# Taking the first norm's sums of squares from a second, untransposed copy of the input

## The chip, the cores and the metric

One core of one Trainium2 chip. The metric is device time in microseconds (us) of one execution; the kernel before takes 523.28 us (median of 3 runs, 523.22 to 523.72). Everything is float32; the large matmuls run in a split form described below.

## The reference, cut to what matters

One layer of an encoder trunk on 512 tokens of width 1024:

```
h    = rms_norm(x, attn_norm_g)            # x * rsqrt(mean(x*x) + 1e-6) * g, per token
proj = h @ w_in                            # 1024 x 2560: [xr | gate | q | k | v]
xr   = conv4(xr) -> RG-LRU scans, * gelu(gate);  q, k, v -> dilated attention
x    = x + concat(norm(y_rnn), norm(y_attn)) @ w_out
x    = x + relu(norm(x) @ w_up)^2 @ w_down
out  = rms_norm(x, final_norm_g)
```

The change concerns the first line alone: the 512 numbers mean(x*x), one per token.

## The kernel before, in words

**Layout.** The host passes x twice: transposed with weights beside it (`xw0`, `xw`: eight pieces of 128 channels x 512 tokens, each with 384 columns of `w_in`), and with tokens on partitions (`xn`, eight pieces of 128 tokens x 512 channels), which the kernel before reads only later, for the residual. The projection puts channels on the contracted dimension, so it works on the transposed copy. The norm's factor per token (`rstd`) is not multiplied into x; it is applied to the projections when they leave PSUM. So the matmuls can begin before the sums of squares are known.

**Split matmuls.** Every large product is three matmuls of a high part and a low part (`mm3`, lines 312 to 314). The high part is a rounded copy (ScalarE, line 247 for a chunk of weights, `conv_hi`; VectorE for a few chunks, line 245), the low part is the difference (VectorE, line 269, `conv_lo`).

**The opening.** `cvx(k)` (lines 353 to 367) splits piece k of x and of the weights beside it. `sq(k)` (line 372) squares the piece on ScalarE, `addsq` (line 375) adds the squares over the eight pieces on VectorE. TensorE meanwhile runs three output tiles of the projection over k (`pxr`, lines 453 and 458); after the first triple of the last k it turns the 128 x 512 sum of squares with four transposes (`turned`, line 430). VectorE sums the turned tile along its rows (line 435), scales it (line 414), POOL raises it to the power -1/2 (line 417, `rcol`), TensorE spreads it to a row with four more transposes (`row_tile`, line 409), ScalarE copies it out of PSUM (line 423, `rrow`, which is `rstd`).

**What hangs on `rstd`.** `conv_a(t)` (lines 496, 498) scales a `pxr` tile by it and begins the width-4 convolution, `conv_b(t)` (lines 503 to 505) ends it; both for t = 0 to 3. VectorE runs them one after the other. `lru_gates` (lines 528, 532) then multiplies each convolved tile by four small gate matrices on TensorE, in order of t, and ScalarE evacuates them. Between, TensorE runs the fourth `pxr` tile (`xmm`, chunk 3 of the weights) and the gate projections (`pp`, chunk 4 onward, one chunk a tile).

**Order.** TensorE, ScalarE, VectorE and POOL issue in the order of the program (a hand-written schedule). The transfers of SyncE's queue (SP) are placed by the framework's scheduler: seven pieces of x and weights, the vectors `vt`, piece 7 (it reuses the buffer of piece 0, so it waits until that piece has been read), weight chunks 3, 4 and 5 (`emit_dma`, line 230; three buffers, which pieces 4 to 6 of x occupy first), then the four gate matrices (line 320), then chunks 6 and 7 as buffers come free. ScalarE splits chunk 3, then chunk 5, and only then copies out `rrow`; chunk 4's high part is VectorE's.

Of the kernel before, what the change touches and what calls it, by code (L numbers as in the profile page):

```python
# [12 lines left out]
FT = mybir.dt.float32  # L13
FR = mybir.dt.float32r
AF = mybir.ActivationFunctionType
OP = mybir.AluOpType

P = 128
S = 512
D = 1024  # L20
KD = D // P
# [77 lines left out]
def hybrid_kernel(ctx: ExitStack, tc, xw0, xw, xn, w_in, w_v, w_out, w_up, w_dn, gates, vecs, bias, fg, out):  # L99
    nc = tc.nc  # L100
    consts = ctx.enter_context(tc.tile_pool(name="consts", bufs=1))
# [7 lines left out]
    act = nc.scalar.activation  # L109
    stt = nc.vector.scalar_tensor_tensor  # L110
    NG = 45

    def g_(name, dt=FT, shape=(P, S)):
        return work.tile(list(shape), dt, name=name, tag="g", bufs=NG)

    def small(name, w):
        return work.tile([P, w], FT, name=name, tag="sm%d" % w, bufs=8)

    def ps_(name, tag):
        return psum.tile([P, S], FT, name=name, tag=tag, bufs={"pj": 4, "gs": 2, "et": 2}[tag])  # L120

    def f(t):
        return t.bitcast(FT)


    vt = consts.tile([P, NVEC], FT, name="vt")
# [6 lines left out]
    ident = consts.tile([P, P], FT, name="ident")  # L133
# [10 lines left out]
    def softplus_consts():  # L144
        ts, tt = nc.gpsimd.tensor_scalar, nc.gpsimd.tensor_tensor
        lam = vt[:, VEC["lam"]:VEC["lam"] + 8]
        e8, sp, z, z2, pl = [small(n, 8) for n in ("e8", "sp8", "z8", "z28", "pl8")]
        cneg = consts.tile([P, 8], FT, name="cneg")
        chalf = consts.tile([P, 8], FT, name="chalf")
        stt(e8, lam, -1.0, lam, op0=OP.mult, op1=OP.max)  # L150
        nc.vector.tensor_scalar(sp, lam, -1.0, 0.0, op0=OP.mult, op1=OP.max)
        yield
        act(e8, e8, AF.Exp, scale=-1.0)
        yield
        nc.vector.tensor_scalar(z, e8, 2.0, None, op0=OP.add)
        nc.vector.reciprocal(z, z)
        tt(z, z, e8, op=OP.mult)
        tt(z2, z, z, op=OP.mult)
        ts(pl, z2, 1.0 / 19, 1.0 / 17, op0=OP.mult, op1=OP.add)
        for c in (15, 13, 11, 9, 7, 5, 3, 1):  # L160
            if c == 7:
                yield
            tt(pl, pl, z2, op=OP.mult)
            ts(pl, pl, 1.0 / c, None, op0=OP.add)
        tt(pl, pl, z, op=OP.mult)
        ts(pl, pl, 2.0, None, op0=OP.mult)
        tt(sp, pl, sp, op=OP.add)
        ts(cneg, sp, -LRU_C, None, op0=OP.mult)
        ts(chalf, sp, 0.5 * LRU_C, None, op0=OP.mult)
        yield cneg, chalf  # L170

    spc = softplus_consts()
# [38 lines left out]
    def source(c):  # L211
        if not isinstance(c, tuple):
            return c
        if c[0] == "o":
            return oblock(c[1])
        return ublock(*c[:3]) if len(c) == 4 else wblock(*c)
# [9 lines left out]
    def emit_dma():  # L226
        if plain:
            i = plain.popleft()
            r = stream.tile([P, 1024], FT, name="wraw", tag="wraw", bufs=3)
            nc.sync.dma_start(r, source(chunks[i]))  # L230
            raws[i] = r
# [86 lines left out]
    def gate_load(t):  # L318
        gwr[t] = g_("gwr", shape=(P, 4 * DH))
        nc.sync.dma_start(gwr[t], gates[t])  # L320


    h_hi = big.tile([P, KD, S], FR, name="h_hi", tag="bigA")
    h_lo = big.tile([P, KD, S], FR, name="h_lo", tag="bigB")

    XW, XG = S + 3 * P, S + KD
    ag = consts.tile([P, KD], FT, name="ag")
    xwt, w3 = [], []
    for k in range(KD):
        if 4 <= k < 7:  # L330
            xwt.append(stream.tile([P, 1024], FT, name="wraw", tag="wraw", bufs=3)[:, :XW])
        else:
            xwt.append(work.tile([P, 1024], FT, name="tw", tag="tw", bufs=4)[:, :XW if k else XG + 3 * P])
        if k == 0:
            nc.sync.dma_start(xwt[0][:, :XG], xw0[:, :XG])
            nc.sync.dma_start(xwt[0][:, XG:], xw0[:, XG:])
            nc.gpsimd.tensor_copy(ag, xwt[0][:, S:XG])
            w03 = g_("w03")[:, :P]
            nc.sync.dma_start(w03, w_in[3][:, :P])
        else:  # L340
            nc.sync.dma_start(xwt[k], xw[k - 1])
        if k == 6:
            nc.sync.dma_start(vt, vecs)

    sqx = {}

    def cvx(k):
        x, w = xwt[k][:, :S], xwt[k][:, S if k else XG:]
        g = ag[:, k:k + 1] if k else xwt[0][:, S:S + 1]
        hi, lo = g_("w3h", FR), g_("w3l", FR)  # L350
        if k < 2:
            c = (2 * P, 3 * P)[k]
            act(h_hi[:, k, :c], x[:, :c], AF.Copy, scale=g)
            nc.vector.tensor_scalar(h_hi[:, k, c:], x[:, c:], g, None, op0=OP.mult)
            if k == 0:
                nc.vector.tensor_copy(hi[:, :2 * P], w[:, :2 * P])
                act(hi[:, 2 * P:3 * P], w[:, 2 * P:], AF.Copy)
            else:
                nc.vector.tensor_copy(hi[:, :3 * P], w)
        else:  # L360
            act(h_hi[:, k, :], x, AF.Copy, scale=g)
            act(hi[:, :3 * P], w, AF.Copy)
        stt(h_lo[:, k, :], x, g, f(h_hi)[:, k, :], op0=OP.mult, op1=OP.subtract)
        nc.vector.tensor_tensor(lo[:, :3 * P], w, f(hi)[:, :3 * P], op=OP.subtract)
        if k == 0:
            act(hi[:, 3 * P:], w03, AF.Copy)
            nc.vector.tensor_tensor(lo[:, 3 * P:], w03, f(hi)[:, 3 * P:], op=OP.subtract)
        w3.append((hi, lo))

    def sq(k):  # L370
        sqx[k] = g_("sqx")
        act(sqx[k], xwt[k][:, :S], AF.Square)

    def addsq(k):
        nc.vector.tensor_tensor(sqx[0], sqx[0], sqx.pop(k), op=OP.add)

    cvx(0)
    sq(0)
    for k in range(1, KD):
        cvx(k)  # L380
        if 5 <= k < 7:
            next(spc)
        sq(k)
        if k >= 2:
            addsq(k - 1)
    emit_dma()
    for t in range(4):
        gate_load(t)
    emit_dma()
    addsq(7)  # L390
    emit_dma()

    def hk(k):
        return (h_hi[:, k, :], h_lo[:, k, :])

    def wk(c, k):
        if c < 3 or (c, k) == (3, 0):
            return tuple(t[:, c * P:(c + 1) * P] for t in w3[k])
        hi, lo = splits[c]
        return (hi[:, k * P:(k + 1) * P], lo[:, k * P:(k + 1) * P])  # L400
# [11 lines left out]
    def rstd_cols(ssc, n):  # L412
        v = small("rv", 4)
        nc.vector.tensor_scalar(v, ssc, 1.0 / n, EPS, op0=OP.mult, op1=OP.add)
        r = consts.tile([P, 4], FT, name="rcol_%d" % st["rc"])
        st["rc"] += 1
        nc.gpsimd.tensor_tensor(r, v, mhalf, op=OP.pow)
        return r

    def row_tile(cols, tag):  # L420
        pr = rows_of(lambda tt: fan(cols, tt, 1, P), tag)
        r = g_("rrow")
        act(r, pr, AF.Copy)
        return r


    def turned(ss, tag):
        pc = ps_("pcs", tag)
        for tt in range(4):
            nc.tensor.transpose(pc[:, tt * P:(tt + 1) * P], ss[:, tt * P:(tt + 1) * P], ident)  # L430
        return pc

    def row_sums(pc):
        c = small("cs", 4)
        nc.vector.tensor_reduce(c, pc.rearrange("p (t c) -> p t c", t=4), axis=mybir.AxisListType.X, op=OP.add)
        return c

    def col_sums(ss):
        t, u, c = g_("cst"), small("cu", 16), small("cs", 4)
        nc.vector.transpose(t, ss)  # L440
# [8 lines left out]
    for k in range(KD):  # L449
        if k < 2:  # L450
            for i, (a, b) in enumerate(((0, 0), (0, 1), (1, 0))):
                for t in range(3):
                    nc.tensor.matmul(pxr[t], lhsT=wk(t, k)[a], rhs=hk(k)[b], start=i == 0 and k == 0, stop=False)
            if k == 0:
                mm3(pxr[3], wk(3, 0), hk(0), True, False)
            continue
        for t in range(3):
            mm3(pxr[t], wk(t, k), hk(k), False, k == KD - 1)
            if k == KD - 1 and t == 0:
                sqt = turned(sqx[0], "et")  # L460


    bt = consts.tile([P, 2 * NBC], FT, name="bt")
# [198 lines left out]
    def xmm(ks):  # L662
        for k in ks:
            mm3(pxr[3], wk(3, k), hk(k), False, k == KD - 1)

    conv_hi(3)
    conv_lo(3)
    rcol = rstd_cols(row_sums(sqt), D)
    conv_hi(4)
    conv_hi(5)  # L670
    nc.gpsimd.dma_start(bt, bias)
    conv_lo(4)
    xmm(range(1, 3))
    rstd = row_tile(rcol, "et")
    conv_a(0, pxr[0])
    conv_a(1, pxr[1])
# [1 line left out]
    cneg, chalf = next(spc)  # L678
    conv_b(0)
    act(warm, epsb, AF.Sigmoid)  # L680
    xmm(range(3, KD))
    conv_a(2, pxr[2])
    conv_a(3, pxr[3])
    conv_hi(6)
# [58 lines left out]
    for n, (k, tt) in enumerate(steps):  # L743
        c = C_V + k // 2
        if k == 0:
            pv[tt] = ps_("pv", vtag[tt])
        hi, lo = splits[c]
# [42 lines left out]
    et, en, zs = {}, {}, {}  # L790
# [479 lines left out]
    for w in OSEQ:  # L1270
        for i in range(4):
            tt, k = i // 2, i % 2
# [267 lines left out]
    for half in range(2):  # L1540
# [169 lines left out]
        for j in range(7 * NQ):  # L1710
            _, w, q = seq[j]
# [124 lines left out]
```

## Time and profile before

| | before |
|---|---|
| median of 3 runs | 523.28 us (523.22 to 523.72) |
| the profiled execution's own time | 522.93 us |
| its span, first to last instruction | 521.1 us |
| TensorE busy | 514.8 us, 99% of the span |
| VectorE, ScalarE, POOL busy | 430.5, 352.3, 66.2 us |
| granted TensorE clock, mean | 0.999 of full speed |
| DMA | 105.15 MB, mean 202 GB/s |

The profile is one execution. Times within it count from its first instruction. 1.8 us of the profiled execution's time lie outside its span. PE is TensorE's matmuls, PEld its weight loads, DVE VectorE, ACT ScalarE, POOL GpSimd, SPq the queue that SyncE issues. An idle time in brackets stands for the engine just before the instruction, with what ended it.

### The profile page before, as it was taken

To read this page: it belongs to the slowest core of one execution; us is meant where nothing else is said; L and a number is where in the kernel's file an instruction comes from. 1 tells how busy PE (TensorE), PEld (TensorE's weight loads), DVE (VectorE), ACT (ScalarE), POOL (GpSimd) and SP (SyncE) were. 2 spreads that over 40 slices of the span, in tenths; PEclk is the share of its full clock that TensorE was granted. 3 is DMA by queue.
4 is the path that set the end of the run, shared out by engine and by line. 5 is a ranking of instruction groups with operands and counts; after the bars stand their busy time and mean duration, and the time that the engine had idled before them with its cause. 6 is when DMAs were issued, how large, how long until landed. Compare 5 with 4: busy or idle time off the path is not lost.

```text
span 521.1 us, 8223 instructions
## 1 busy us (share of the span) xinstructions
PE 514.8 (99%) x3021; PEld 444.0 (85%) x3021; DVE 430.5 (83%) x667; ACT 352.3 (68%) x571; POOL 66.2 (13%) x89
## 2 busy tenths in 40 slices
PE   9999999999999999999999999999999999999995
PEld 7857888887778788899999888889999999888884
DVE  6998985887789998898789987789766978986885
ACT  7579946777759757685568655675667577655655
POOL 0183000000010410000300412001100300231000
PEclk9999999999999999999999999999999999999999
DMA  8736555477376799847695899967986496799704
GB/s 289 224 92 198 160 155 181 117 203 209 82 250 234 196 206 285 309 148 170 154 209 158 212 275 276 309 259 165 302 259 164 117 229 211 154 290 257 198 1 162
DMA packets 40329, 105.15 MB, mean 202 GB/s; under 512 B 5056, under 2 KB 13376, under 8 KB 40288
## 3 DMA queue, kind: packets, MB, share of 16 engines
q1 hardware_dynamic: 32448, 78.07, 44.9%
q0 software_dynamic: 7696, 26.32, 27.3%
q8 instruction: 24, 0.39, 0.3%
q10 hardware_dynamic: 144, 0.23, 0.1%
q14 instruction: 17, 0.14, 0.1%
HBM read 95.59 MB, written 4.29 MB: 192 GB/s over the span
## 4 chain that ended last, share of the span: by engine, by line
PE 99%; ACT 0%; DVE 0%; issue 0%
PE pu L312 10%; PE pu L314 10%; PE pu L313 10%; PE pd L314 10%; PE pd L312 10%; PE pd L313 10%; PE pqk L312 3%; PE pqk L314 3%; PE pqk L313 3%; PE pwo L312 3%; PE pwo L314 3%; PE pwo L313 3%; PE pav L941 2%; PE pt L841 2%; PE ps L805 2%; PE pp L312 1%
## 5 line engine op out<-in xcount | busy, mean ns | idle before, releaser
L269 DVE TENSOR_TENSOR wlo<-wraw,whi 128x1024 fp32r<-128x1024 f32 x71 | 86.5, 1219 | 22.2 <-ACT whi L247 22.0
L247 ACT ACTIVATE whi<-wraw 128x1024 fp32r<-128x1024 f32 x67 | 70.8, 1058 | 36.8 <-PE pd L314 19.0
L313 PE MATMUL pd<-wlo,ah 128*128 128x512 f32 (+1 forms) x195 | 75.2, 386 | 0.0
L312 PE MATMUL pd<-whi,ah 128*128 128x512 f32 (+1 forms) x195 | 75.2, 386 | 0.0
L314 PE MATMUL pd<-whi,al 128*128 128x512 f32 (+1 forms) x195 | 75.2, 386 | 0.0
L313 PE MATMUL pu<-hl,whi 128*128 128x256 f32 x224 | 63.4, 283 | 0.0
L314 PE MATMUL pu<-hh,wlo 128*128 128x256 f32 x224 | 63.4, 283 | 0.0
L312 PE MATMUL pu<-hh,whi 128*128 128x256 f32 x224 | 63.4, 283 | 0.0
L312 PE MATMUL pu<-h2h,whi 128*128 128x256 f32 (+1 forms) x200 | 60.1, 301 | 0.0
L313 PE MATMUL pu<-h2l,whi 128*128 128x256 f32 (+1 forms) x200 | 60.0, 300 | 0.0
L314 PE MATMUL pu<-h2h,wlo 128*128 128x256 f32 (+1 forms) x200 | 60.0, 300 | 0.0
L269 DVE TENSOR_TENSOR wlo<-tw,whi 128x1024 fp32r<-128x1024 f32 x37 | 45.2, 1222 | 17.6 <-ACT whi L247 17.6
L247 ACT ACTIVATE whi<-tw 128x1024 fp32r<-128x1024 f32 x38 | 40.1, 1058 | 24.9 <-PE pd L314 6.3
L312 PEld LDWEIGHTS pu<-hh,whi 128*128 128x128 f32 x224 | 43.0, 192 | 0.0
L313 PEld LDWEIGHTS pu<-hl,whi 128*128 128x128 f32 x224 | 43.0, 192 | 0.0
L314 PEld LDWEIGHTS pu<-hh,wlo 128*128 128x128 f32 x224 | 43.0, 192 | 0.0
L247 ACT ACTIVATE whi<-ts 128x1024 fp32r<-128x1024 f32 x24 | 25.5, 1061 | 25.9 <-PE pd L314 18.4
L313 PEld LDWEIGHTS pd<-wlo,ah 128*128 128x128 f32 x195 | 36.6, 188 | 7.4
L314 PEld LDWEIGHTS pd<-whi,al 128*128 128x128 f32 x195 | 36.6, 188 | 7.4
L312 PEld LDWEIGHTS pd<-whi,ah 128*128 128x128 f32 x195 | 36.6, 188 | 7.3
L314 PEld LDWEIGHTS pu<-h2h,wlo 128*128 128x128 f32 x200 | 38.3, 191 | 1.3
L313 PEld LDWEIGHTS pu<-h2l,whi 128*128 128x128 f32 x200 | 38.3, 191 | 1.3
(283 smaller groups left out, 1221.4 us busy)
## 6 DMA issues: line engine op xcount, KB each, us to landing
wraw<-in_w_up_dram SPq DMA_DIRECT2D x25, 512.0 KB, 4.0
ts<-in_w_dn_dram POOLq DMA_DIRECT2D x24, 512.0 KB, 12.9
wraw<-in_w_dn_dram SPq DMA_DIRECT2D x24, 512.0 KB, 10.4
tw<-in_w_up_dram SPq DMA_DIRECT2D x15, 512.0 KB, 5.3
tw<-in_w_up_dram POOLq DMA_DIRECT2D x15, 512.0 KB, 7.5
wraw<-in_w_in_dram SPq DMA_DIRECT2D x13, 512.0 KB, 3.5
ts<-in_w_dn_dram SPq DMA_DIRECT2D x8, 512.0 KB, 8.6
tw<-in_w_dn_dram SPq DMA_DIRECT2D x8, 512.0 KB, 6.8
```

The source lines that it names most:

```text
L247: act(hi, raws[i], AF.Copy)
L269: nc.vector.tensor_tensor(lo, r, f(splits[i][0]), op=OP.subtract)
L312: nc.tensor.matmul(o, lhsT=a[0], rhs=b[0], start=bool(first), stop=False, skip_group_check=on)
L313: nc.tensor.matmul(o, lhsT=a[0], rhs=b[1], start=False, stop=False, skip_group_check=on)
L314: nc.tensor.matmul(o, lhsT=a[1], rhs=b[0], start=False, stop=bool(last), skip_group_check=on)
L805: nc.tensor.matmul(pss[e][:, :NK], lhsT=qs_[p, a][r, P * qt:P * qt + P], rhs=kks[p][r, b, w:w + NK], start=i == 0, stop=i == 2)
L841: nc.tensor.transpose(pt[:, i * P:(i + 1) * P], en[h][qt][:, k:k + P], ident)
L941: nc.tensor.matmul(pav[p][a, co], lhsT=vs[:, jt, h * DH:(h + 1) * DH], rhs=et[h, jt][:, ci], start=jt == 0 and i == 0, stop=jt == 3 and i ...
```

## The change

The squares are taken from `xn`, where a token's channels lie along one partition, so that ScalarE's accumulator gives the sum of each row as it squares. Eight transfers of 128 x 512 (256 KB each) bring `xn` in, eight squares give eight columns of `ss8`, one small addition gives the four columns that `rstd_cols` takes. The squares of the transposed pieces, their seven additions, the four transposes and the row sum go. On SP the order is now written out: pieces 1 to 6, `vt`, piece 7, `xn` 0 to 3, chunk 3, `xn` 4 to 7, chunk 4, the four gate matrices, chunk 5. ScalarE squares `xn` 0 to 3 after piece 7 is split, and 4 to 7 after chunk 3's high part. One more step of the fourth `pxr` tile (k = 3) stands ahead of `row_tile`.

```diff
+    with tc.manual_schedule(engines={nc.sync.engine}):
+        for k in range(7):
+            load_xw(k)
+        nc.sync.dma_start(vt, vecs)
+        xs = [g_("xs") for _ in range(8)]
+        ss8 = consts.tile([P, 8], FT, name="ss8")
+        def load_xs(i):
+            nc.sync.dma_start(xs[i], xn[i])
+        def sq(i):
+            act(xs[i], xs[i], AF.Square, accum_out=ss8[:, 4 * (i % 2) + i // 2:4 * (i % 2) + i // 2 + 1])
...
-    cvx(0)
-    sq(0)
-    for k in range(1, KD):
-        cvx(k)
-        if 5 <= k < 7:
-            next(spc)
-        sq(k)
-        if k >= 2:
-            addsq(k - 1)
-    emit_dma()
-    for t in range(4):
-        gate_load(t)
-    emit_dma()
-    addsq(7)
-    emit_dma()
+        for k in range(KD):
+            cvx(k)
+            if k == 0:
+                load_xw(7)
+                for i in range(4):
+                    load_xs(i)
+            if 5 <= k < 7:
+                next(spc)
+        emit_dma()
+        for i in range(4, 8):
+            load_xs(i)
+        emit_dma()
+        for t in range(4):
+            gate_load(t)
+        emit_dma()
+        for i in range(4):
+            sq(i)
...
         for t in range(3):
             mm3(pxr[t], wk(t, k), hk(k), False, k == KD - 1)
-            if k == KD - 1 and t == 0:
-                sqt = turned(sqx[0], "et")
...
     conv_hi(3)
     conv_lo(3)
-    rcol = rstd_cols(row_sums(sqt), D)
+    for i in range(4, 8):
+        sq(i)
+    ssx = small("cs", 4)
+    nc.vector.tensor_tensor(ssx, ss8[:, :4], ss8[:, 4:], op=OP.add)
+    rcol = rstd_cols(ssx, D)
     conv_hi(4)
     conv_hi(5)
     nc.gpsimd.dma_start(bt, bias)
     conv_lo(4)
-    xmm(range(1, 3))
+    xmm(range(1, 4))
     rstd = row_tile(rcol, "et")
...
-    xmm(range(3, KD))
+    xmm(range(4, KD))
```

## Rows read from the trace of the kernel before

**Rows 1.** The page: busy time by engine, and the chain that ended last.

```profile
PE 514.8 (99%) x3021; PEld 444.0 (85%) x3021; DVE 430.5 (83%) x667; ACT 352.3 (68%) x571; POOL 66.2 (13%) x89
...
PE 99%; ACT 0%; DVE 0%; issue 0%
```

**Rows 2.** Timeline of PE: start, us, engine, line, operation, tiles, shapes, count.

```profile
9.65 0.39 PE L312 MATMUL pxr<-h_hi,w3h 128*128 128x512 f32 x1
...
20.57 0.60 PE L430 MATMUL pcs<-ident,sqx 128*128 128x128 f32 x4
20.93 0.48 PE L312 MATMUL pxr<-h_hi,w3h 128*128 128x512 f32 x1
...
22.40 0.40 PE L312 MATMUL pxr<-h_hi,whi 128*128 128x512 f32 x1
...
23.78 0.60 PE L409 MATMUL prow<-ident,rcol 128*128 128x128 f32 x4
...
27.66 0.39 PE L312 MATMUL pp<-h_hi,whi 128*128 128x512 f32 x1
...
32.88 0.39 PE L314 MATMUL pp<-h_hi,wlo 128*128 128x512 f32 x1
```

**Rows 3.** Lines of DVE and ACT, 6 to 20 us: count, busy us, mean ns.

```profile
L375 DVE TENSOR_TENSOR sqx<-sqx 128x512 f32<-128x512 f32 x7 | 4.8, 684 | 0.1
...
L372 ACT ACTIVATE sqx<-tw 128x512 f32<-128x512 f32 x5 | 3.1, 617 | 0.0
```

**Rows 4.** Activations that also give a row sum: lines of ACT, 90 to 160 us.

```profile
L822 ACT ACTIVATE e<-e,mn 128x416 f32<-128x416 f32 x32 | 20.1, 629 | 11.7 <-DVE mn L821 11.7
...
L822 ACT ACTIVATION_READ_ACCUMULATOR e<-e,mn 128x1 f32 x32 | 6.0, 186 | 0.0
```

**Rows 5.** Timeline of ACT, 16.9 to 44 us.

```profile
16.91 0.62 ACT L372 ACTIVATE sqx<-tw 128x512 f32<-128x512 f32 x1
17.43 1.05 ACT L247 ACTIVATE whi<-wraw 128x1024 fp32r<-128x1024 f32 x1
21.76 1.06 ACT L247 ACTIVATE whi<-wraw 128x1024 fp32r<-128x1024 f32 x1 [3.27 <-DMA wraw<-in_w_in_dram]
24.42 0.60 ACT L423 ACTIVATE rrow<-prow 128x512 f32<-128x512 f32 x1 [1.60 <-PE prow L409]
...
34.32 9.36 ACT L532 ACTIVATE ga<-pg,vt 128x512 f32<-128x512 f32 x16 [2.26 <-PE pg L528]
```

**Rows 6.** Timeline of SP's issues and POOL's power.

```profile
6.22 0.33 SPq L341 DMA_DIRECT2D tw<-in_xw_dram  x1
...
17.09 0.33 SPq L230 DMA_DIRECT2D wraw<-in_w_in_dram  x1
...
22.26 1.34 POOL L417 TENSOR_TENSOR rcol<-rv,mhalf 128x4 f32<-128x4 f32 x1 [18.52 <-DVE rv L414]
```

**Rows 7.** DMA issues: count, KB each, median us to landing (piece 7, gates, chunk 5).

```profile
tw<-in_xw_dram SPq DMA_DIRECT2D x1, 448.0 KB, 7.4
...
gwr<-in_gates_dram SPq DMA_DIRECT2D x4, 128.0 KB, 4.5
...
wraw<-in_w_in_dram SPq DMA_DIRECT2D x1, 512.0 KB, 4.6
```

**Rows 8.** Windows: us, busy (x) by engine, PEclk, DMA share, GB/s.

```profile
4.40:9.50 5.10, 5.10 (x22) 4.02 (x22) 3.87 (x9) 3.51 (x7) 0.00 (x0) 1.00 1.00 386
...
19.00:21.70 2.70, 2.70 (x15) 2.25 (x14) 2.60 (x4) 0.00 (x0) 0.00 (x0) 1.00 0.96 332
```

**Rows 9.** Timeline of DVE, 25 to 40 us.

```profile
25.05 1.29 DVE L496 TENSOR_TENSOR xr<-pxr,rrow 128x512 f32<-128x512 f32 x2 [1.09 <-ACT rrow L423]
...
36.70 0.75 DVE L505 SCALAR_TENSOR_TENSOR xc<-xr,vt,xc 128x511 f32<-128x511 f32 x1
```

**Rows 10.** Timeline of PE's weight loads (PEld), 38 to 41 us.

```profile
38.40 0.15 PEld L528 LDWEIGHTS pg<-xc,gwr 64*64 64x64 f32 x4 [0.28 <-issue]
...
40.22 0.19 PEld L312 LDWEIGHTS pp<-h_hi,whi 128*128 128x128 f32 x1 [0.81 <-ACT ga L532]
```

More of the change, by code (lines that the diff above doesn't have):

```diff
@@ L328, in hybrid_kernel, with load_xw @@
     xwt, w3 = [], []
-    for k in range(KD):
+    w03 = g_("w03")[:, :P]
+    def load_xw(k):
         if 4 <= k < 7:
@@ L337, in hybrid_kernel @@
             nc.gpsimd.tensor_copy(ag, xwt[0][:, S:XG])
-            w03 = g_("w03")[:, :P]
             nc.sync.dma_start(w03, w_in[3][:, :P])
@@ L341, in hybrid_kernel @@
             nc.sync.dma_start(xwt[k], xw[k - 1])
[L342 to L354, printed above, removed]
-            if k == 0:
[L356 to L375, printed above, removed]
-    cvx(0)
-    sq(0)
-    for k in range(1, KD):
-        cvx(k)
-        if 5 <= k < 7:
-            next(spc)
-        sq(k)
-        if k >= 2:
-            addsq(k - 1)
-    emit_dma()
-    for t in range(4):
-        gate_load(t)
-    emit_dma()
-    addsq(7)
-    emit_dma()
+    with tc.manual_schedule(engines={nc.sync.engine}):
[8 more added lines that the diff above has]
+            act(xs[i], xs[i], AF.Square, accum_out=ss8[:, 4 * (i % 2) + i // 2:4 * (i % 2) + i // 2 + 1])
+        def cvx(k):
+            x, w = xwt[k][:, :S], xwt[k][:, S if k else XG:]
+            g = ag[:, k:k + 1] if k else xwt[0][:, S:S + 1]
+            hi, lo = g_("w3h", FR), g_("w3l", FR)
+            if k < 2:
+                c = (2 * P, 3 * P)[k]
+                act(h_hi[:, k, :c], x[:, :c], AF.Copy, scale=g)
+                nc.vector.tensor_scalar(h_hi[:, k, c:], x[:, c:], g, None, op0=OP.mult)
+                if k == 0:
+                    nc.vector.tensor_copy(hi[:, :2 * P], w[:, :2 * P])
+                    act(hi[:, 2 * P:3 * P], w[:, 2 * P:], AF.Copy)
+                else:
+                    nc.vector.tensor_copy(hi[:, :3 * P], w)
+            else:
+                act(h_hi[:, k, :], x, AF.Copy, scale=g)
+                act(hi[:, :3 * P], w, AF.Copy)
+            stt(h_lo[:, k, :], x, g, f(h_hi)[:, k, :], op0=OP.mult, op1=OP.subtract)
+            nc.vector.tensor_tensor(lo[:, :3 * P], w, f(hi)[:, :3 * P], op=OP.subtract)
+            if k == 0:
+                act(hi[:, 3 * P:], w03, AF.Copy)
+                nc.vector.tensor_tensor(lo[:, 3 * P:], w03, f(hi)[:, 3 * P:], op=OP.subtract)
+            w3.append((hi, lo))
+        for k in range(KD):
+            cvx(k)
+            if k == 0:
+                load_xw(7)
[12 more added lines that the diff above has]
+            sq(i)
@@ L424, in row_tile @@
         return r
[L427 to L436, printed above, removed]
     def col_sums(ss):
```

## The prediction, made before the change was run

> **What bounds the kernel now.** First the page: TensorE is busy for 99% of the span, and 99% of the chain that ended last is TensorE's [rows 1]. So an instruction taken from TensorE is worth its own length, work taken from another engine is worth nothing by itself, and a wait put in front of TensorE costs its full length.
>
> Then the timeline of TensorE around the change [rows 2]. The gate projections show the steady pace: from 27.66 to 32.88 us 23 matmuls start, one each 0.227 us. That pace holds from 9.65 us, when the third piece of x begins, so the opening has no gap left that a faster ScalarE or VectorE could close; its squares (8 of 617 ns) and additions (7 of 684 ns) already lie beside TensorE [rows 3]. The four transposes begin at 20.57 us.
>
> Last, what must be ready for TensorE: `rcol` for `row_tile` at 23.78, and the convolved tiles for the gate matmuls after 33 us.
>
> **What goes.** The transposes hold TensorE from 20.57 to 20.93, 0.36 us. The 12 matmuls up to 23.78 then take 2.85 us where 12 x 0.227 is 2.72, so 0.13 us more is lost in getting back to pace [rows 2]. Together **-0.49 us**. The squares (8 x 0.617 = 4.9 us of ScalarE) and additions (7 x 0.684 = 4.8 us of VectorE) are worth nothing on the path. They do free both engines earlier: pieces 2 to 7 will be split as they land.
>
> **What comes.** Eight transfers of 256 KB, eight squares with row sums, one tiny addition for the row sum of the turned tile. A square with its sum costs between 0.617 us [rows 3] and 0.617 + 0.186 = 0.803 us, the second being the reading of the accumulator [rows 4]. I take 0.72, since the activations here overlap by 0.1 us: one of 0.62 us from 16.91 is followed at 17.43 [rows 5]. ScalarE has room: the last four take 2.9 us of the 3.27 us that it now waits ahead of chunk 5 [rows 5].
>
> **What moves.** Here lies the risk: the order on SP. Piece 7 was issued at 6.22 and landed 7.4 us later, at 13.6 [rows 6, 7], at the end of an unbroken burst. SP's transfers then had a pause until buffers came free; chunk 5, issued at 17.09, took 4.6 us and landed at 21.7 [rows 6, 7]. Now the queue behind piece 7 never empties: `xn` 0 to 3 fill the pause, and chunk 5, now behind the gates too, stands behind 8 x 256 + 2 x 512 + 4 x 128 KB. With its own 512 KB that is 4096 KB, 4.19 MB. Two rows price it. At the burst's 386 GB/s (DMA share 1.00) it takes 10.9 us: chunk 5 lands at 24.5. At 332 GB/s of the stretch with chunk 5 and the gates (share 0.96) it takes 12.6 us: 26.2 [rows 8]. I take **24.9**, near the first, because the new queue is unbroken like the burst; the slower stretch contains starts after idle.
>
> The others in that queue, at 386 GB/s: chunk 3 (1.57 MB behind piece 7) lands at 17.7, its split ends on ScalarE at 19.0 and on VectorE near 20.2, and TensorE asks for it at 22.40 - 0.49 = 21.9 [rows 2]: covered. Chunk 4 (3.15 MB) lands at 21.8, is split by 24, and is needed at 27.2 [rows 2]: covered. `xn` 7 (2.62 MB) lands at 20.4; four squares end near 21.6, the addition and scaling take some 0.4 us, POOL 1.34 us [rows 6]: `rcol` by 23.5. `row_tile` now has three more matmuls ahead, so TensorE reaches it at 23.78 - 0.49 + 3 x 0.227 = 23.97 [rows 2]: covered by 0.5 us. At 332 GB/s `rcol` comes at 24.6, and TensorE would stand 0.6 us there. Chunks 6 and 7 land near 26 and 28, and the first is split at 31: covered.
>
> **Who waits for chunk 5.** ScalarE, in order: it splits chunk 5 (1.06 us) before it copies out `rrow` [rows 5]. Today it waits 3.27 us for chunk 5, and still has 1.60 us to spare before `rrow` at 24.42 [rows 5]. With chunk 5 at 24.9, `rrow` starts 1.0 us later (1.06 less the overlap), at 25.9: **1.5 us late**. Behind it stands all of VectorE's work: the scaling of the `pxr` tiles that starts at 25.05 after 1.09 us idle, then the convolutions back to back, the last ending at 36.70 + 0.75 = 37.45 [rows 9]. No idle time shows in between, so the last tile now ends at 38.95.
>
> TensorE needs that tile for the last quarter of the gate matmuls, at 38.40 today [rows 10], at 37.91 without the transposes. The next projection starts at 40.22, 1.82 us after, of which about 0.1 us is a wait for ScalarE's evacuation [rows 10]. So TensorE resumes at 38.95 + 1.72 = 40.67 instead of 40.22: **+0.45 us against before**; say +0.5 with the wake-up. In one formula, the change is chunk 5's landing minus 24.4, and never under -0.49. Earlier, the first `pp` tile waits until VectorE has emptied a bank, at 25.05 + 1.5 + 0.65 = 27.2, just when TensorE wants it (27.66 - 0.49) [rows 2, 9]; a stall there is part of the same lateness and not added.
>
> After that the lateness does not spread: ScalarE's evacuations follow TensorE, not VectorE, and start at 34.32 after 2.26 us idle [rows 5].
>
> **Against a page.** The burst ran at 386 GB/s over 5 us with the DMA engines busy throughout [rows 8]. The Trainium skill, "DMA: Bandwidth & Descriptors", section "Where 436 GB/s comes from", has loads from HBM bound by about 358 GB/s a core. By that rule the 4.19 MB take 11.7 us, chunk 5 lands at 25.3, and the change is an estimated +0.9. The trace does not agree: it moved more than that without a break. That would still lie inside the forecast; the sum above does not use the rule.
>
> **The forecast**, against the profiled execution: 522.93 + 0.5 = 523.4. The median of the runs is 0.35 above that execution, so the figure is 523.28 + 0.5 = **523.8 us**. A measurement of this kernel can tell about 0.2%, 1.05 us, from no change; this lies within.
>
> **Rivals.** *Hidden transfers (chance 0.23).* The queue gets chunk 5 there by about 24, or VectorE's chain has slack that I don't see. Then only the transposes count: -0.49, 522.8 us. For it: ScalarE has 1.60 us to spare today. Against it: 4.19 MB in 10.4 us would be 403 GB/s, above the burst.
>
> *Chunk 5 late by more (0.25; slower).* One mechanism: ScalarE stands at chunk 5's split, `rrow` behind it, VectorE behind that, TensorE at the last quarter of the gate matmuls. It decides from a landing at 25.45 on, where 25.45 - 24.4 is 1.05 us. At 332 GB/s it is 26.2, +1.8 us, 525.1 us. For it: the slower row is the one with these very transfers, and every such transfer waits for its last part. Against it: that stretch follows a pause.
>
> *The sums late instead (0.04).* `xn` 7 comes so late that `row_tile` holds TensorE. At 332 GB/s that is 0.6 us, but chunk 5 then lands later still and hides it, so the time is that of the rival above unless chunk 5 happens to be early; alone it gives -0.49 + 0.6 = +0.1, 523.4 us.
>
> *Faster by over 0.2% (0.03)* would need a wait of TensorE elsewhere to vanish; 6.3 us of the span are without a matmul (521.1 less 514.8) [rows 1], none of it visible near the change.
>
> **How the numbers follow.** The forecast (landing between 24 and 25.4) has 0.45. The range, 522.7 to 525.1, reaches from the hidden case to the slow bound and takes in the bounds of both unknown prices, leaving out about one in ten. Slower by over 0.2%: 0.25. Faster: 0.03. The rest, 0.72, is within 0.2%: the forecast, the hidden transfers and the late sums.
>
> **What would show it.** Right: no matmul at the place of the transposes; ScalarE idle until about 24.9 before chunk 5's split; `rrow` near 25.9; VectorE's convolutions 1.5 us later; TensorE waiting up to a microsecond for `xc` or a bank between 27 and 39 us, then everything in step. Wrong: chunk 5 landing before 24 or after 25.5; TensorE standing at `row_tile`; TensorE not waiting although the convolutions are late; a difference that arises after 60 us.

## The result, and the profile after

| | before | after |
|---|---|---|
| median of 17 runs | 523.11 us (522.73 to 523.72) | 523.91 us (523.38 to 525.36) |
| ratio, 95% interval | | 1.0017 [1.001, 1.0025] |
| the profiled execution's span | 521.1 us | 522.3 us |
| VectorE, ScalarE busy | 430.5, 352.3 us | 425.7, 353.5 us |

The change costs 0.8 to 0.9 us: too little to count as slower by the 0.2% of the prediction, and near the forecast of +0.5. The page of after answers to [rows 1]: four matmul records fewer, 5 us of VectorE's work gone, and TensorE as full as it was.

```profile
PE 515.6 (99%) x3017; PEld 444.4 (85%) x3017; DVE 425.7 (81%) x660; ACT 353.5 (68%) x579; POOL 66.2 (13%) x89
...
PE 99%; ACT 0%; issue 0%; DVE 0%
```

ScalarE's timeline after, against [rows 5]:

```profile
14.57 0.62 ACT L356 ACTIVATE xs<-xs 128x512 f32<-128x512 f32 x1
15.10 0.19 ACT L356 ACTIVATION_READ_ACCUMULATOR xs<-xs 128x1 f32 x1
15.19 0.62 ACT L356 ACTIVATE xs<-xs 128x512 f32<-128x512 f32 x1
...
20.93 0.62 ACT L356 ACTIVATE xs<-xs 128x512 f32<-128x512 f32 x1
...
25.17 1.06 ACT L247 ACTIVATE whi<-wraw 128x1024 fp32r<-128x1024 f32 x1 [3.53 <-DMA wraw<-in_w_in_dram]
26.14 0.58 ACT L429 ACTIVATE rrow<-prow 128x512 f32<-128x512 f32 x1
```

All eight squares are done by 21.6 us. Then ScalarE stands for 3.53 us until chunk 5 has landed, and `rrow` follows its split at once. Before, `rrow` came at 24.42, 1.60 us after ScalarE had become idle.

VectorE's timeline after, against [rows 9]: the row sums, the first scaling, the last convolution.

```profile
21.67 0.16 DVE L664 TENSOR_TENSOR cs<-ss 128x4 f32<-128x4 f32 x1 [1.23 <-ACT xs L356]
...
26.75 1.29 DVE L489 TENSOR_TENSOR xr<-pxr,rrow 128x512 f32<-128x512 f32 x2 [2.86 <-ACT rrow L429]
...
38.39 0.75 DVE L498 SCALAR_TENSOR_TENSOR xc<-xr,vt,xc 128x511 f32<-128x511 f32 x1
```

The scaling starts 1.70 us later than before, the last convolution 1.69 us later: the lateness of `rrow` goes down VectorE's chain undiminished.

TensorE's timeline after, against [rows 2, 10]:

```profile
22.73 0.39 PE L312 MATMUL pxr<-h_hi,whi 128*128 128x512 f32 x1
...
24.77 0.60 PE L415 MATMUL prow<-ident,rcol 128*128 128x128 f32 x4
...
27.98 0.39 PE L312 MATMUL pp<-h_hi,whi 128*128 128x512 f32 x1
...
33.51 5.38 PE L521 MATMUL pg<-xc,gwr 64*64 64x512 f32 x48
39.24 1.95 PE L521 MATMUL pg<-xc,gwr 64*64 64x512 f32 x16 [0.35 <-issue]
41.12 0.50 PE L312 MATMUL pp<-h_hi,whi 128*128 128x512 f32 x1
```

In this execution TensorE is 0.33 us behind before at chunk 3 (22.73 against 22.40) and 0.32 at the first `pp` (27.98 against 27.66): its opening, told of below, was 0.80 us behind at 13 us, and without the four transposes it made up 0.48 of that. But it is not this lateness that counts in the end. The last quarter of the gate matmuls starts at 39.24, where before had it at 38.40: 0.84 us behind. The row puts the gap down to issue, but the last convolution ends at 38.39 + 0.75 = 39.14, 0.1 us ahead; in every kernel below that has this gap, the matmuls resume 0.10 or 0.11 us after that convolution ends. From here the two traces run in step, but for a part between 103 and 177 us that the experiments isolate. So most of the time is lost at one place, and it is the place that the prediction named.

### The profile page after: what moved, and what is told of

Read it like the earlier page. It is cut to its first block, busy times and chain, and to the rows that moved or that the text cites. A ratio compares the mean times of both kernels' runs of the same rounds, so it can differ in the third digit from the quotient of the medians.

```text
span 522.3 us, 8213 instructions
## 1 busy us (share of the span) xinstructions
PE 515.6 (99%) x3017; PEld 444.4 (85%) x3017; DVE 425.7 (81%) x660; ACT 353.5 (68%) x579; POOL 66.2 (13%) x89
## 4 chain that ended last, share of the span: by engine, by line
PE 99%; ACT 0%; issue 0%; DVE 0%
PE pu L314 10%; PE pu L312 10%; PE pu L313 10%; PE pd L314 10%; PE pd L313 10%; PE pd L312 10%; PE pqk L312 3%; PE pqk L314 3%; PE pqk L313 3%; PE pwo L312 3%; PE pwo L314 3%; PE pwo L313 3%; PE pav L938 2%; PE pt L838 2%; PE ps L802 2%; PE pp L312 1%
## 5 line engine op out<-in xcount | busy, mean ns | idle before, releaser
L269 DVE TENSOR_TENSOR wlo<-wraw,whi 128x1024 fp32r<-128x1024 f32 x71 | 86.5, 1220 | 25.7 <-ACT whi L247 25.3
```

What stands on the lines that cost most here:

```text
L269: nc.vector.tensor_tensor(lo, r, f(splits[i][0]), op=OP.subtract)
```

## The experiments

The theory: the change's loss is chunk 5's landing, by ScalarE's order, and the gain of the four transposes is hidden by that wait. The rivals: the loss is made elsewhere (the late opening, the drift after 100 us), or the transposes were worth nothing.

**Two ways to take the wait away.** e1 transfers chunk 5 ahead of the gate matrices; e2 leaves the transfers and lets ScalarE split chunk 5 after `rrow`.

```diff
 # e1
         emit_dma()
+        emit_dma()
         for t in range(4):
             gate_load(t)
-        emit_dma()
 # e2
     conv_hi(4)
-    conv_hi(5)
...
     act(warm, epsb, AF.Sigmoid)
+    conv_hi(5)
```

> The changed kernel with one edit on SP: chunk 5 is issued ahead of the four gate matrices instead of behind them. Theory (the late chunk 5 holds ScalarE, rrow behind it, VectorE's convolutions behind that, TensorE at the last quarter of the gate matmuls): chunk 5 lands about 1.4 us earlier, near 23.7, the wait at the gate matmuls goes, and only the removed transposes count: about 0.5 us under the kernel before, ratio 0.999. Rival A (the extra 2 MB or the squares cost by contention, wherever they stand): as the changed kernel, 0.8 us over before, ratio 1.0016. Rival B (the full TensorE clock came 2 us later in the opening of the changed kernel's profile, and that is the loss): the loss stays, since the opening is the same.

> The changed kernel with one edit on ScalarE: the split of chunk 5 stands behind the copy of rrow and the first two convolution starts; all transfers stay where they are. Theory: chunk 5 lands as late as before (25.2), but rrow no longer waits for it: rrow near 24.7, no wait at the gate matmuls, about 0.5 us under the kernel before, ratio 0.999. Rival A (contention or the added work): as the changed kernel, ratio 1.0016. Rival B (the opening's clock): no difference from the changed kernel.

Measured: e1 523.51 us, ratio 1.0005 [0.9996, 1.0014]; e2 523.16 us, 1.0001 [0.9992, 1.0009]. ScalarE and TensorE of e1:

```profile
23.66 1.06 ACT L247 ACTIVATE whi<-wraw 128x1024 fp32r<-128x1024 f32 x1 [2.67 <-DMA wraw<-in_w_in_dram]
25.39 0.60 ACT L429 ACTIVATE rrow<-prow 128x512 f32<-128x512 f32 x1 [0.67 <-PE prow L415]
...
33.50 7.10 PE L521 MATMUL pg<-xc,gwr 64*64 64x512 f32 x64
```

The same of e2:

```profile
25.09 0.60 ACT L429 ACTIVATE rrow<-prow 128x512 f32<-128x512 f32 x1 [3.99 <-PE prow L415]
29.40 1.05 ACT L247 ACTIVATE whi<-wraw 128x1024 fp32r<-128x1024 f32 x1
...
33.19 7.10 PE L521 MATMUL pg<-xc,gwr 64*64 64x512 f32 x64
```

In both, `rrow` waits for TensorE's `prow` and no longer for a transfer, and the 64 gate matmuls stand as one group of 7.10 us, as before the change. In after they are 48 and 16 with a gap. Since e2 moves no transfer and e1 no instruction of an engine, what they have in common is the wait. The times are less clear than the traces: both intervals end below the 1.0016 of rival A (and of B, which expected no change), but both begin above the 0.999 that the theory expected. 0.29 us of that shortfall is found below, under the drift; how much of the rest is the scatter of the openings was not measured.

**The transposes put back.** e3 is after with four transposes of a piece of x at the old place, e4 the same on top of e1; nothing reads the result.

```diff
+            if k == KD - 1 and t == 0:
+                pc = ps_("pcs", "et")
+                for tt in range(4):
+                    nc.tensor.transpose(pc[:, tt * P:(tt + 1) * P], xwt[7][:, tt * P:(tt + 1) * P], ident)
```

> The changed kernel with the four removed transposes of TensorE put back at their old place (of piece 7 of x; their result is not used). Theory: TensorE waits for the convolutions later anyway, so 0.49 us of work ahead of that wait costs nothing: as the changed kernel, 0.8 us over before, ratio 1.0016. Rival (gains and losses add up): 0.49 us more, 1.3 us over before, ratio 1.0025.

> Chunk 5 ahead of the gates, and the four transposes put back (result not used). Theory: with the wait gone the transposes cost their 0.49 us again: equal to the kernel before within 0.2 us, ratio 1.000, and 0.5 us over the run with the gates last alone. Rival (transposes hidden anyway): equal to the run with the gates last alone.

Measured: e3 523.83 us, 1.0014 [1.0005, 1.0022]; e4 523.83 us, 1.0009 [1.0001, 1.0018]. TensorE of e3:

```profile
20.95 0.60 PE L457 MATMUL pcs<-ident,tw 128*128 128x128 f32 x4
...
39.31 1.95 PE L525 MATMUL pg<-xc,gwr 64*64 64x512 f32 x16 [0.36 <-issue]
```

With the four transposes TensorE resumes at 39.31, without them at 39.24, and chunk 5's split starts 0.07 us later too (25.24 against 25.17): the wait for chunk 5 hides them. Where the wait is gone, e4 is 0.0004 above e1, about 0.2 us; the intervals overlap, so the times alone don't show what the transposes are worth, and e4's interval misses the 1.000 that was expected (the drift below adds 0.29 us). The traces do show it. From the last matmul ahead of the transposes' place to the gate matmuls, e4:

```profile
20.32 0.39 PE L314 MATMUL pxr<-h_hi,w3l 128*128 128x512 f32 x1
...
33.17 7.10 PE L525 MATMUL pg<-xc,gwr 64*64 64x512 f32 x64
```

The same matmul of e1, whose gate matmuls start at 33.50 (above):

```profile
21.13 0.39 PE L314 MATMUL pxr<-h_hi,w3l 128*128 128x512 f32 x1
```

That is 12.85 us with the transposes, as in before (20.34 to 33.19), and 12.37 without: they cost 0.48 us, and without the wait TensorE gets all of it.

**The wait made longer.** e8 is after with two more transfers of 256 KB ahead of chunk 5, which nothing reads.

```diff
             gate_load(t)
+        for i in range(2):
+            nc.sync.dma_start(g_("more"), xn[i])
         emit_dma()
```

> The changed kernel with two more transfers of 256 KB (xn 0 and 1 once more, not used) on SP ahead of chunk 5. Theory (the change is chunk 5's landing less 24.4): 0.52 MB at 386 GB/s puts chunk 5 back by 1.36 us to 26.5, rrow, the convolutions and the last quarter of the gate matmuls with it, one for one: 1.3 us over the changed kernel, 2.1 us over before, ratio 1.0041. Rival (the wait for chunk 5 is not the bound): as the changed kernel, ratio 1.0017.

Measured: 525.55 us, 1.0045 [1.0033, 1.0058]. ScalarE and TensorE of e8:

```profile
26.14 1.06 ACT L247 ACTIVATE whi<-wraw 128x1024 fp32r<-128x1024 f32 x1 [4.62 <-DMA wraw<-in_w_in_dram]
27.11 0.58 ACT L431 ACTIVATE rrow<-prow 128x512 f32<-128x512 f32 x1
...
40.22 1.95 PE L523 MATMUL pg<-xc,gwr 64*64 64x512 f32 x16 [0.66 <-ACT ga L527]
```

Chunk 5 is split 0.97 us later than in after, and TensorE resumes 0.98 us later: one for one. The time is 0.0028 above after's, 1.5 us from five runs; the intervals leave room for 0.98. Why the 524 KB took 0.97 us and not 1.36 is read from the transfers, below.

**The drift after 100 us.** The change also moves memory: `ss8` is a new tile and `w03` is allocated earlier, so later tiles lie elsewhere. e5 is e1 and e6 is after, each with these two put back; e7 is before with both moved and nothing else (its `ss8` is set to zero and not read).

```diff
 # e5, e6
-    w03 = g_("w03")[:, :P]
+    w03 = None
...
     def load_xw(k):
+        nonlocal w03
...
+            w03 = g_("w03")[:, :P]
...
-        ss8 = consts.tile([P, 8], FT, name="ss8")
+        ss8 = small("ss8", 8)
 # e7
     xwt, w3 = [], []
+    w03 = g_("w03")[:, :P]
+    ss8 = consts.tile([P, 8], FT, name="ss8")
+    nc.vector.memset(ss8, 0.0)
...
-            w03 = g_("w03")[:, :P]
```

> Chunk 5 ahead of the gates, and the memory of SBUF laid out as in the kernel before: ss8 takes a spare small buffer and w03 is allocated after the first piece of x, so that the weights and h stand at their old addresses (in the runs so far the new 32-byte ss8 moved everything behind it by 32 bytes, and the order of two pools was exchanged). Theory of the layout: the 1 to 3 ns that each matmul between 100 and 170 us took longer in all runs so far (together 0.3 us) go; with the wait gone too, 0.5 us under the kernel before, ratio 0.999. Rival (the growth after 100 us has another cause, as transfers or engines that run beside the matmuls): as with the gates last alone, ratio 1.0000 to 1.0005, and the same growth in the trace.

> The changed kernel with the old layout of SBUF alone; order of transfers as changed. Theory of the layout: the wait at the gate matmuls stays (0.85 us late there in the trace), the growth of 0.3 us after 100 us goes: 0.5 us over before, ratio 1.0010. Rival: no difference from the changed kernel, ratio 1.0017.

> The kernel before with the layout of the changed kernel alone: an unused ss8 of 32 bytes a partition, set to zero once, and w03 allocated first. Theory of the layout: the matmuls between 100 and 170 us take 0.3 us longer in sum, ratio 1.0006. Rival (the layout does nothing): ratio 1.0000 and no growth in the trace.

Measured: e5 523.04 us, 0.9996 [0.9987, 1.0005]; e6 524.11 us, 1.0016 [1.0007, 1.0025]; e7 523.34 us, 1.0005 [0.9996, 1.0014]. The same two places of TensorE's program, first in before:

```profile
102.92 0.82 PE L841 MATMUL pt<-ident,e 128*128 128x128 f32 x6
...
177.31 0.39 PE L312 MATMUL pwo<-whi,oh 128*128 128x512 f32 x1
```

In after:

```profile
103.79 0.82 PE L838 MATMUL pt<-ident,e 128*128 128x128 f32 x6
...
178.47 0.39 PE L312 MATMUL pwo<-whi,oh 128*128 128x512 f32 x1
```

In e7:

```profile
102.83 0.82 PE L843 MATMUL pt<-ident,e 128*128 128x128 f32 x6
...
177.50 0.39 PE L312 MATMUL pwo<-whi,oh 128*128 128x512 f32 x1
```

In e6:

```profile
103.89 0.82 PE L840 MATMUL pt<-ident,e 128*128 128x128 f32 x6
...
178.28 0.39 PE L312 MATMUL pwo<-whi,oh 128*128 128x512 f32 x1
```

The stretch takes 74.39 us in before and e6, 74.68 in after, 74.67 in e7. The other kernels fall in with them: 74.67 or 74.68 in e1 to e4 and e8, which have the placement of after, 74.38 to 74.40 in both executions of e5, in e9 and in e10, which have that of before. So **0.29 us comes with the placement in memory** and has nothing to do with the norm: before gets it with the placement of after, and after loses it with that of before. The times are less clear: e7 is above before by about the 0.3 us that the trace shows, within its interval; e6 isn't below after, and its interval holds the 1.0010 of the theory and the 1.0017 of the rival alike.

**All repairs together.** e9 is e2 with the placement of before; e10 has e1's order as well. e5 was run once more beside them.

> The change with chunk 5's split after rrow (as e2) and the memory layout of before (as e5). If the wait for chunk 5 and the layout are the two terms, both are gone and only the transposes' gain is left: no jump at the gate matmuls and no growth between 100 and 170 us, ratio to before 0.999 (0.998 to 1.000). If the layout is worth nothing in the times: as e2, 1.000.

> The change with chunk 5 transferred ahead of the gates (as e1), its split after rrow (as e2) and the layout of before. The theory expects the same as e9, ratio 0.999 (0.998 to 1.000), since either removes the wait; a rival in which rrow is still late by something else than chunk 5 expects it lower than e9 by 0.0005 or more.

> Kernel e5 once more, on the chip of these runs: ratio 0.9995 (0.9987 to 1.0005), within 0.0005 of e9 and e10.

Measured: e9 522.65 us, 0.9993 [0.9984, 1.0002]; e10 523.21 us, 1.0000 [0.9991, 1.0009]; e5 again 522.71 us, 0.9990 [0.9981, 0.9999]. ScalarE and TensorE of e10, the execution whose opening ran most like that of before:

```profile
24.49 0.60 ACT L431 ACTIVATE rrow<-prow 128x512 f32<-128x512 f32 x1 [3.38 <-PE prow L417]
...
32.59 7.10 PE L523 MATMUL pg<-xc,gwr 64*64 64x512 f32 x64
```

The gate matmuls start at 32.59, against 33.19 in before: 0.60 us earlier, of which 0.12 stood already in the opening, at 8 us. The 0.48 that is left is the price of the transposes. The profiled span of e10 is 520.5 us against 521.1. The median spans of these runs agree: 520.9 us for e9 and for this run of e5 (521.2 for its first), 521.0 for e10, 521.4 for before. In the times the gain is at the edge of what can be told: the four ratios without the long wait and with the placement of before (e5 twice, e9, e10) are 0.9990 to 1.0000, and only one interval ends below 1. e10 was not lower than e9, as the theory said and its rival did not. e5 came within 0.0005 of e9, as expected, but not of e10 (0.9990 against 1.0000); why was not found. So the best version of the change gains up to some 0.5 us, and none is shown to beat the kernel before clearly.

The two repairs are not equal. With e1's order chunk 5 did not always come as early as in e1. In the second execution of e5:

```profile
24.23 1.06 ACT L247 ACTIVATE whi<-wraw 128x1024 fp32r<-128x1024 f32 x1 [2.57 <-DMA wraw<-in_w_in_dram]
...
32.86 7.39 PE L523 MATMUL pg<-xc,gwr 64*64 64x512 f32 x64
```

`rrow` follows that split at once, and the gate matmuls take 7.39 us instead of 7.10: a rest of the wait is left. e2's order, which takes chunk 5 out of `rrow`'s way, shows none in e2, e9 or e10.

## Why the prediction was right, point by point

**What goes: right.** -0.49 us for the transposes; 0.48 in e10. The squares and additions were worth nothing on the path, as said.

**The sums: right, with a smaller price.** A square with its row sum starts every 0.62 us (14.57, 15.19), where 0.72 was taken between 0.617 and 0.803: half of the reading's 0.19 us lies beside the next square. A square without a sum was followed after 0.52 us [rows 5], so the sum costs 0.10 us. `rcol` was forecast by 23.5. POOL's timeline after, against [rows 6]:

```profile
22.19 1.34 POOL L423 TENSOR_TENSOR rcol<-rv,mhalf 128x4 f32<-128x4 f32 x1 [18.41 <-DVE rv L420]
```

It ends at 23.53. `row_tile` was forecast at 23.97; it is at 24.77 in after because of the late opening, and TensorE did not stand there. The 0.5 us by which the prediction held it covered are fewer, though: in e6, whose opening was early, `rcol` ends at 23.90 and TensorE waits for it some 0.1 us, to 23.96. The wait for chunk 5 hides this, so the rival of the late sums is out as a cause of the loss.

**Chunk 5's landing: the mechanism right, the term 0.25 us too small.** Forecast 24.9, measured just ahead of 25.17. The windows of after, with the columns of [rows 8]:

```profile
13.60:21.70 8.10, 8.10 (x38) 6.70 (x37) 3.39 (x6) 7.04 (x20) 0.00 (x0) 1.00 1.03 386
21.70:23.40 1.70, 1.70 (x9) 1.41 (x8) 1.63 (x4) 0.00 (x0) 1.21 (x1) 1.00 1.03 398
23.40:25.10 1.70, 1.70 (x10) 1.40 (x9) 0.49 (x1) 0.00 (x0) 0.89 (x2) 1.00 0.82 276
```

The unbroken queue keeps the burst's 386 GB/s for 8 us, as the sum had it, and 398 after. What it had too small was the end: in the last 1.7 us before the landing the rate falls to 276 GB/s, at a DMA share of 0.82 (239 and 242 GB/s in e3 and e6). By the three rows 4.27 MB had moved by 25.1, against the 4.19 MB of the sum, so some bytes of other transfers lie in between as well. By the 358 GB/s of the Trainium skill, "DMA: Bandwidth & Descriptors", section "Where 436 GB/s comes from", the prediction had estimated a landing at 25.3, nearer to the 25.17 than the forecast. The trace agrees with that time and not with the rate: 386 and 398 GB/s stand in rows of nearly 10 us, and the rate drops only in the last two. The Trainium skill's "HBM Reference", section "Specifications (TRN2)", has a core that streams alone, as here, well above that share; with this the rows agree. In e8, where more transfers stand around chunk 5, the same windows show:

```profile
23.40:25.10 1.70, 1.70 (x12) 1.41 (x11) 0.39 (x1) 0.00 (x0) 0.79 (x2) 1.00 1.02 414
25.10:26.10 1.00, 1.00 (x6) 0.83 (x5) 0.00 (x0) 0.00 (x0) 0.00 (x0) 1.00 1.04 401
```

There is no slow end there, which is more than enough for the 0.39 us by which the two added transfers cost less than 1.36 (524 KB at 386 GB/s): between 23.4 and 25.1, 138 GB/s more over 1.7 us are 235 KB, 0.6 us at 386 GB/s. Why the rate falls in after was not tried.

**Who waits: right.** "The change is chunk 5's landing minus 24.4", set against TensorE's resuming at the last quarter, which before has at 38.40 [rows 10]:

| kernel | chunk 5's split starts | formula | TensorE resumes | measured |
|---|---|---|---|---|
| after | 25.17 | +0.77 | 39.24 | +0.84 |
| e3 | 25.24 | +0.84 | 39.31 | +0.91 |
| e6 | 25.27 | +0.87 | 39.35 | +0.95 |
| e8 | 26.14 | +1.74 | 40.22 | +1.82 |
| e5, second execution | 24.23 | -0.17 | 38.30 | -0.10 |

It is 0.07 to 0.08 us low in all five, beside the 0.05 given to the wake-up. e6 also settles the rival of the late opening: it opened 0.9 us ahead of after and resumes no earlier. At the next projection the lateness of after is a little larger, 0.90 us (41.12 against 40.22): the prediction gave that projection 1.72 us from the end of the last convolution, and it took 1.98 (39.14 to 41.12). It had counted on saving the 0.1 us of waiting for ScalarE's evacuation, which was not saved (1.88 us from the resuming, against 1.82 in before). The stall at the first `pp` tile, which the prediction put at 27.2 and didn't add, shows where TensorE comes early enough or the split late enough. TensorE in e6:

```profile
27.60 0.50 PE L312 MATMUL pp<-h_hi,whi 128*128 128x512 f32 x1 [0.22 <-DVE xr L491]
```

In e8:

```profile
28.47 0.50 PE L312 MATMUL pp<-h_hi,whi 128*128 128x512 f32 x1 [0.70 <-DVE xr L491]
```

It is indeed part of the same lateness: both kernels resume at the last quarter as near the formula as the others, and no later.

**Against the median.** +0.84 and +0.29 make 1.13 us, and the spans of the two profiled executions differ by 1.2; the medians differ by 0.8. The execution of before that was profiled lies 0.3 us below its median span (521.1 against 521.4), that of after 0.3 above its own (522.3 against 522.0). For before the scatter of the openings, told of below, can make this; for after, where the wait swallows it, the cause is open.

**What the prediction did not have.** It named a difference after 60 us as a sign that it was wrong. There is one, the 0.29 us of placement. The missed terms all have one sign: 0.25 us at chunk 5's landing, some 0.15 from there to the next projection, 0.29 of placement. On the profiled executions they make the change 1.2 us where +0.5 was forecast. That the medians differ by only 0.8, and that 523.91 lies so near the 523.8 of the forecast, is in part luck: of the scatter, and of the three runs of before from which the forecast started, whose median of 523.28 is 0.17 above that of all 17.

## What to carry to other kernels

When a change fills a pause in a queue, look for the transfer at the queue's far end and for the engine that will wait for it in order: here 2 MB of new transfers cost nothing where they were used and 0.8 us where a split stood, by program order, ahead of something urgent. Moving that split behind the urgent instruction gives it back without any other edit; moving the transfer ahead of others that are not yet needed gives back most or all of it, depending on how early it then lands. Work taken from the bounding engine shortens nothing as long as the engine then waits for something with a date of its own.

## What the runs showed of the hardware that was not expected

**The opening does not run alike twice.** The first matmuls of before:

```profile
4.44 1.18 PE L453 MATMUL pxr<-h_hi,w3h 128*128 128x512 f32 x3
5.45 0.85 PE L453 MATMUL pxr<-h_lo,w3h 128*128 128x512 f32 x3
```

And of after:

```profile
4.47 1.62 PE L448 MATMUL pxr<-h_hi,w3h 128*128 128x512 f32 x3
5.89 1.32 PE L448 MATMUL pxr<-h_lo,w3h 128*128 128x512 f32 x3
```

The same three matmuls take 1.18 us in one and 1.62 in the other (0.93 in e6). What differs is the moment at which TensorE gets its full clock. In after its matmuls start 0.43 us apart up to 6.74 and 0.23 us apart from 7.05 on; in before they are 0.23 us apart from 4.98 on. The trace's own record of the granted clock begins with the full 2.4 GHz at 6.90 us in after and at 4.95 in before. It has no entry ahead of that, so a window's column reads 1.00 there too; the pace, nearly half, is that of the lower level, 1.2 GHz. In both kernels TensorE had run sixteen small warm-up matmuls from 0.8 us on.

The two executions of e5, one kernel, have the full clock from 6.44 and from 4.86, so the edit alone doesn't decide it, and what sets the moment was not found. Whether the edit shifts the odds is open: with the opening of before it came at 4.95 and 4.11 (e7), in the eleven other traces between 3.69 (e10) and 6.90, seven times after 6 us. Where nothing later waits for a transfer this scatter goes straight into the time (e1, with the full clock from 6.82, ends late by it in its profile); in after it is swallowed by the wait for chunk 5.

**Placement in memory.** Two tiles moved, and 75 us of matmuls take 0.29 us longer. Groups of TensorE's matmuls between 106 and 128 us, first in before:

```profile
L805 PE MATMUL ps<-kk,qh 64*128 64x416 f32 x16 | 2.3, 359 | 0.0
```

In e7:

```profile
L807 PE MATMUL ps<-kk,qh 64*128 64x416 f32 x16 | 2.4, 363 | 0.0
```

It is 4 ns each (359 to 363), without a wait that the profile shows. Which of the moved tiles does it, and against what, was not tried.
